# A decoder block on one core: the first loads of a product issued inside the unit before it, and its left factors written in portions between the weight splits

## The chip, the cores and the metric

The program runs on one core of a Trainium2 chip. TensorE (PE in the profile) multiplies matrices, VectorE (DVE), ScalarE (ACT) and GpSimd (POOL) work elementwise, and SyncE (SP) issues nearly all DMA transfers. Each of these works through its own list of instructions in order, and waits on semaphores for the others. The metric is the device time of one execution, in microseconds (us).

## The reference

One hybrid decoder block over 512 positions with 2048 features, in float32. Cut to what is computed:

```
h = rmsnorm(x, norm_mix_g);  z = h @ w_in                    # q, k, v, forget gates, zu, zv
attn = forgetting_attention(q, k, v, log_sigmoid(f + b_f))   # 8 heads, causal softmax
gm   = gelu(zu) * (tril(w_s) @ layernorm(gelu(zv)) + b_s)    # chunks of 128 positions
merged = concat(rmsnorm(attn, attn_out_g), rmsnorm(gm, gmlp_out_g))
x = x + merged @ w_out
h2 = rmsnorm(x, norm_ffn_g)
x = x + square(relu(h2 @ w_ff1)) @ w_ff2                     # 2048 -> 8192 -> 2048
return rmsnorm(x, norm_final_g)
```

The change is at the seam between `merged @ w_out` and `h2 @ w_ff1`, the first product of the channel MLP.

## The kernel before

Every float32 operand is written as a high part that TensorE takes exactly and a low part, the rest: ScalarE casts the high part, VectorE subtracts it from the source. A product is then three matmuls, high by high, high by low, low by high.

**Projection units.** The projections are cut into units of 128x512 weight tiles; `run_units` walks through their steps. A step prepares the weights of three steps ahead (load, `wh` on ScalarE, `wl` on VectorE), issues 12 matmuls of 128x512 into four PSUM tiles, calls the unit's `done` after its last step, and then `tick()`, which gives background tasks their turn: a task is a generator, and the number that it yields is how many ticks it sleeps. The last eight units multiply by `w_out`: `oa0` to `oa3` for the attention half, then `og0` to `og3`, whose `g_done(c)` adds both halves to x and so makes the features 512c to 512c+511 of the block's middle x, called `oa[c]`.

**The first channel product** (`first_product`, 448 groups) is a Strassen-Winograd product with seven partial products P1 to P7. Its left factors are seven forms (A11, A12, A22, S1 to S4) of the middle x, made for every c by `scale_x2(c)` (4 scalings on ScalarE, 4 sums on VectorE) and `make_forms(c, which)` (for each form one cast `L699` on ScalarE and one subtraction `L700` on VectorE). Its right factors are blocks of `w_ff1`, loaded by `load(u, j)` in four DMAs: `b11`, `r`, and the sums `t1` and `t3`, which the background task `sums_task` has made earlier (lines `L668` to `L674`) and put in DRAM. `prepare(i)` splits one weight block for one group: cast `fh` (`L723`) and subtraction `fl` (`L724`). A group is 12 matmuls of 128x256 on `L791`. The order of the groups in one j is P5, P1, P6, P2, P7, P4, P3. The groups of j = 0 and 1 read the forms of c = 0 and 1, those of j = 2 the forms of c = 2, those of j = 3 the forms of c = 3. In this text P7' is group P7 of j = 1.

**The seam.** `g_done(3)` first starts `first_product`, whose first part loads the blocks of j = 0 and 1 and prepares three groups; then it reads the four PSUM tiles of `og3` (`L614`, `L615`), scales, and makes the five remaining forms of c = 2 and all seven of c = 3. `turn_x2(c)` is a task that transposes `oa[c]` on TensorE (`px`, `L636`), copies it out on ScalarE and stores it; for c = 2 its first two pieces fall into `og3`, the rest between groups of the first product.

**What sets the order.** TensorE's order is that of the program. On the other engines a scheduler arranges the instructions when the kernel is built, by its own estimate of when operands come. SP's queue is in order too: a DMA that waits for its buffer holds all later ones. The buffers that matter: `t2_pool` (7 tiles; `b11`, `t1`, `t3`, the products of `L614`, the transposed copies), `raw_pool` (4; weights of the units and `r`), `w_pool` (4 `wh` and 4 `wl`, shared by units and groups, so that the split of a group waits for the matmuls of the step or group four before), and the six PSUM tiles of `ps_mm`. By their order of allocation the tile of P5 is the one that `px` 0 of c = 2 used, that of P1 the one of `px` 1; `px` 2 takes the tile `ps_og3_0` and must wait until VectorE has read it in the first `L614`; P6, P2 and P7 take `ps_og3_1`, `_2` and `_3` likewise.

Of the kernel before, what the change touches and what calls it, by code (L numbers as in the profile page):

```python
# [34 lines left out]
def hybrid_block(ctx, tc, xT, win, wf_in, wout, w1, w2, cols_in, ln_in, ws_in, out):  # L35
# [22 lines left out]
    def s8(name, dtype=F32, where=None):  # L58
        return (where or sr_pool).tile([P, 4, 512], dtype, tag="s8", name=name)

    def t2(name, dtype=F32):
        return t2_pool.tile([P, 512], dtype, tag="t2", name=name)
# [7 lines left out]
    def f(ap):  # L70
        return ap.bitcast(F32)
# [110 lines left out]
    tasks = []  # L182

    def start_task(gen, wait=1):
        tasks.append([wait, gen])
# [418 lines left out]
    def g_done(c):  # L604
        def done(ps):
            if c == 3:
                stage["first"] = first_product()
                next(stage["first"])
            if c == 2:
                oa[c] = s8(f"oa{c}")  # L610
            for m in range(4):
                k = 4 * c + m
                o, t = oa[c][:, m, :], t2(f"x2_{k}")
                nc.vector.tensor_tensor(t, ps[m], rG, ALU.mult)  # L614
                nc.vector.tensor_tensor(o, part[k], t, ALU.add)  # L615
            start_task(turn_x2(c), 6)
            scale_x2(c)
            if c < 2:
                make_forms(c, range(NF))
            elif c == 2:  # L620
                make_forms(c, (S1, A11))
            else:
                make_forms(2, (S2, A12, S3, A22, S4))
                make_forms(3, (S1, A11, S2, A12, S3, A22, S4))
        return done

    r2 = const.tile([P, NT], F32, name="r2")
    x2d = [dram.tile([P, NT, 512], F32, name=f"x2d{c}") for c in range(4)]

    def turn_x2(c):  # L630

        for m in range(4):
            xt = t2(f"x2t{c}_{m}")
            pt = mm(f"px{c}_{m}") if c > 1 else ax(f"px{c}_{m}", m % 2)
            for tb in range(NT):
                nc.tensor.transpose(pt[:, tb * P:(tb + 1) * P], oa[c][:, m, tb * P:(tb + 1) * P], ident)  # L636
            nc.scalar.copy(xt, pt)
            nc.sync.dma_start(out=x2d[c][:, :, m * P:(m + 1) * P], in_=xt.rearrange("p (t c) -> p t c", c=P))
            yield 2


    NF = 7
    A11, A12, A22, S1, S2, S3, S4 = range(NF)
# [3 lines left out]
    first = (P5, P1, P6, P2, P7, P4, P3)  # L647
    fac = [dram.tile([NF, P, 1024], F32, name=f"fac{u}") for u in range(NU)]
    stage = {}
    here = tc.keep_in_program_order  # L650

    def pairs(t):
        return t.rearrange("p (q c) -> p q c", q=2)
# [5 lines left out]
    def w1_block(u, j, c, n):  # L659

        return w1[8 * u + 2 * j:8 * u + 2 * j + 2][:, :, c:c + n].rearrange("q p c -> p q c")
# [18 lines left out]
    def scale_x2(c):  # L680
        xg, sx = (s8(f"{n}{c}", F32, sx_pool if c > 1 else None) for n in ("xg", "sx"))
        for m in range(4):
            k = 4 * c + m
            nc.scalar.activation(xg[:, m, :], oa[c][:, m, :], AF.Copy, scale=cols[:, G_FFN + k:G_FFN + k + 1])
        xv = xg.rearrange("p (i r) c -> p r i c", r=2)
        a11, a12, a21, a22 = (xv[:, r, :, t:t + 256] for t in (0, 256) for r in range(2))
        s1, s2, s3, s4 = (pairs(sx[:, i, :]) for i in range(4))
        nc.vector.tensor_tensor(s1, a21, a22, ALU.subtract)
        nc.vector.tensor_tensor(s2, s1, a11, ALU.subtract)
        nc.vector.tensor_tensor(s3, a11, a21, ALU.subtract)  # L690
        nc.vector.tensor_tensor(s4, a12, s2, ALU.add)
        x2g[c] = [a11, a12, a22, s1, s2, s3, s4]

    def make_forms(c, which):
        for i in which:
            if c % 2 == 0:
                forms[i, c // 2] = (sr_pool if c // 2 else sl_pool).tile([P, 4, 2, 256], F32R, tag="s8", name=f"form{i}_{c}")
            t = forms[i, c // 2][:, 2 * (c % 2):2 * (c % 2) + 2]
            nc.scalar.copy(t[:, :, 0, :], x2g[c][i])  # L699
            nc.vector.tensor_tensor(t[:, :, 1, :], x2g[c][i], f(t[:, :, 0, :]), ALU.subtract)  # L700


    def first_product():
# [3 lines left out]
        def load(u, j):  # L707
            if u >= NU:
                return
            b11, t1, t3 = (pairs(t2(f"{n}_{u}{j}")) for n in ("b11", "t1", "t3"))  # L710
            r = raw_pool.tile([P, 2, 512], F32, tag="raw", name=f"r{u}{j}")
            nc.sync.dma_start(out=b11, in_=w1_block(u, j, 0, 256))
            nc.sync.dma_start(out=r, in_=w1_block(u, j, 512, 512))
            nc.sync.dma_start(out=t1, in_=pairs(t1d[u][j]))
            nc.sync.dma_start(out=t3, in_=pairs(t3d[u][j]))
            blocks[u, j] = {P1: b11, P2: r[:, :, 0:256], P3: r[:, :, 256:512], P4: t1, P5: t1, P6: t1, P7: t3}
# [50 lines left out]
                square(b0)  # L767

        load(0, 0)
        load(0, 1)  # L770
        for i in range(3):
            prepare(i)
# [2 lines left out]
        for i, (u, j, p) in enumerate(groups):  # L775
# [9 lines left out]
            for q in range(2):  # L785
                ah, al = a[:, 2 * (j % 2) + q, 0, :], a[:, 2 * (j % 2) + q, 1, :]
                for m in range(2):
                    c = slice(q * 256 + m * P, q * 256 + (m + 1) * P)
# [323 lines left out]
    def g_unit(c):  # L1112
        unit(f"og{c}", wout, 8 * c + 4, 8, G_OUT + 8,
             lambda k: (gm_h[k // 4][:, k % 4, :], gm_l[k // 4][:, k % 4, :]), True, g_done(c))
# [62 lines left out]
```

## Time and profile before

| | |
|---|---|
| three runs | 2018.1 us median (2017.93 to 2018.88) |
| profiled execution | 2020.05 us, of which its trace spans 2018.2 us |
| TensorE busy | 1974.2 us, 98% |
| VectorE busy | 1598.8 us, 79% |
| ScalarE busy | 1052.4 us, 52% |
| GpSimd busy | 84.4 us, 4% |
| granted TensorE clock, mean | 0.991 |

A busy time is the sum of an engine's instructions; matmuls overlap, so TensorE at 98% still tells little about one place. The page's row of 40 slices has TensorE below nine tenths in two neighbouring slices only, the 14th and 15th, and its granted clock below nine tenths in the 15th; a slice is 50.5 us. The views of that stretch, in order of time, say which wait ended last.

### The profile page before, as it was taken

Reading aid. Unit: us, or ns where it says so; the run is one execution under the profiler, and the core shown is the slowest. Engines: PE = TensorE matmul, PEld = TensorE weight load, DVE = VectorE, ACT = ScalarE, POOL = GpSimd, SP = SyncE. Lnnn points to the kernel's source line nnn. Section 1 sums busy time; section 2 is a strip of 40 time slices with the busy share of each in tenths; the row PEclk is TensorE's granted clock in tenths of the full one; section 3 lists DMA queues with packets and bytes.
Section 4 is the critical chain, followed back from the end, with each engine's and each line's share of the span. In section 5 each row is a group of like instructions: output and inputs, shape, how many; then the busy total and the mean of one; then the engine's idle time right before and its main releaser. Section 6 shows DMA issues by size and latency. Waiting matters only on the chain.

```text
span 2018.2 us, 30643 instructions
## 1 busy us (share of the span) xinstructions
PE 1974.2 (98%) x11288; PEld 1729.7 (86%) x11288; DVE 1598.8 (79%) x2400; ACT 1052.4 (52%) x1692; POOL 84.4 (4%) x84
## 2 busy tenths in 40 slices
PE   9999999999999889999999999999999999999997
PEld 6888887888787689999999999997888888888876
DVE  7467566686667579988888888888888998998897
ACT  6344334445424456666666666666644444444455
POOL 5000001100120000000000000000000000000000
PEclk9999999999999989999999999999999999999998
DMA  6465565667766768987667756778956646646632
GB/s 220 150 200 160 192 196 171 206 208 256 235 198 204 241 196 291 323 288 234 196 218 244 234 194 219 242 260 313 354 179 218 229 154 230 242 136 237 246 122 84
DMA packets 226406, 439.91 MB, mean 218 GB/s; under 512 B 18896, under 2 KB 96848, under 8 KB 226128
## 3 DMA queue, kind: packets, MB, share of 16 engines
q1 hardware_dynamic: 225568, 436.09, 64.2%
q8 instruction: 88, 1.44, 0.3%
q10 hardware_dynamic: 432, 1.35, 0.2%
q0 software_dynamic: 256, 0.52, 0.1%
q14 instruction: 62, 0.51, 0.1%
HBM read 337.22 MB, written 100.66 MB: 217 GB/s over the span
## 4 chain that ended last, share of the span: by engine, by line
PE 62%; DVE 3%; issue 1%; DMA 1%; ACT 1%; SPq 0%; POOLq 0%; POOL 0%; DVEq 0%; ACTq 0%
PE q L791 32%; PE bX L1067 16%; PE bZ L1067 8%; PE bY L1067 4%; DVE wl L885 1%; PE ps_og L152 1%; PE ps_og L150 1%; PE ps_og L151 1%; DVE acc L946 0%; DVE acc L913 0%; PE px L636 0%; PE pt L970 0%; DVE acc L914 0%; DMA t<-t1d 0%; DVE raw L878 0%
## 5 line engine op out<-in xcount | busy, mean ns | idle before, releaser
L791 PE MATMUL q<-form,fh 128*128 128x256 f32 x3584 | 650.9, 284 | 8.4 <-ACT fh L723 8.4
L791 PEld LDWEIGHTS q<-form,fh 128*128 128x128 f32 x3584 | 562.7, 193 | 8.8 <-ACT fh L723 8.8
L791 PE MATMUL q<-form,fl 128*128 128x256 f32 x1792 | 510.3, 285 | 8.9 <-DVE fl L724 8.7
L791 PEld LDWEIGHTS q<-form,fl 128*128 128x128 f32 x1792 | 345.9, 193 | 10.6 <-DVE fl L724 10.0
L884 ACT CAST wh<-raw 128x1024 fp32r<-128x1024 f32 x224 | 234.4, 1054 | 222.7 <-PE bX L1067 122.4
L885 DVE TENSOR_TENSOR wl<-raw,wh 128x1024 fp32r<-128x1024 f32 x224 | 271.1, 1223 | 74.1 <-ACT wh L884 73.2
L1067 PE MATMUL bX<-wh,fac 128*128 128x512 f32 x1008 | 323.5, 394 | 3.7 <-ACT k_wl L905 2.1
L724 DVE TENSOR_TENSOR fl<-t,fh 128x512 fp32r<-128x512 f32 x256 | 176.4, 690 | 79.0 <-ACT fh L723 77.8
L1067 PEld LDWEIGHTS bX<-wh,fac 128*128 128x128 f32 x1008 | 190.6, 189 | 52.1 <-ACT k_wh L905 6.3
L723 ACT CAST fh<-t 128x512 fp32r<-128x512 f32 x256 | 158.2, 618 | 122.1 <-PE q L791 87.5
L1067 PE MATMUL bX<-wl,fac 128*128 128x512 f32 x504 | 199.3, 395 | 1.9 <-DVE wl L885 1.9
L1067 PE MATMUL bZ<-wh,fac 128*128 128x512 f32 x512 | 162.8, 389 | 0.0
L1067 PEld LDWEIGHTS bX<-wl,fac 128*128 128x128 f32 x504 | 95.4, 189 | 25.6 <-DVE wl L885 7.1
L1067 PEld LDWEIGHTS bZ<-wh,fac 128*128 128x128 f32 x512 | 96.1, 188 | 19.9
L723 ACT CAST fh<-r 128x512 fp32r<-128x512 f32 x128 | 79.1, 618 | 48.1 <-PE q L791 46.5
L150 PE MATMUL ps_qk<-xh,wh_qk 128*128 128x512 f32 x256 | 101.6, 397 | 0.0
L152 PE MATMUL ps_qk<-xh,wl_qk 128*128 128x512 f32 x256 | 100.0, 391 | 0.0
L151 PE MATMUL ps_qk<-xl,wh_qk 128*128 128x512 f32 x256 | 99.8, 390 | 0.0
L1067 PE MATMUL bZ<-wl,fac 128*128 128x512 f32 x256 | 99.6, 389 | 0.0
L724 DVE TENSOR_TENSOR fl<-r,fh 128x512 fp32r<-128x512 f32 x128 | 88.3, 690 | 11.6 <-ACT fh L723 11.0
L162 ACT ACTIVATE wh_qk<-raw_qk,cols 128x512 fp32r<-128x512 f32 x64 | 46.3, 724 | 94.6 <-PE ps_qk L151 62.9
L163 DVE SCALAR_TENSOR_TENSOR wl_qk<-raw_qk,cols,wh_qk 128x512 fp32r<-128x512 f32 x64 | 47.7, 750 | 59.0 <-ACT wh_qk L162 58.9
(618 smaller groups left out, 3567.3 us busy)
## 6 DMA issues: line engine op xcount, KB each, us to landing
b<-in_w_dram SPq DMA_DIRECT2D x256, 256.0 KB, 4.3
raw<-in_w_dram SPq DMA_DIRECT2D x128, 512.0 KB, 4.9
fac<-fac SPq DMA_DIRECT2D x112, 512.0 KB, 6.2
r<-in_w_dram SPq DMA_DIRECT2D x64, 512.0 KB, 5.5
fac<-fc SPq DMA_DIRECT2D x48, 512.0 KB, 4.2
raw_qk<-in_win_dram SPq DMA_DIRECT2D x32, 512.0 KB, 3.8
t1d<-b SPq DMA_DIRECT2D x64, 256.0 KB, 2.1
t3d<-b SPq DMA_DIRECT2D x64, 256.0 KB, 2.3
```

Of the source, the lines that this page charges most:

```text
L150: nc.tensor.matmul(ps, lhsT=ah, rhs=bh, start=start, stop=False)
L151: nc.tensor.matmul(ps, lhsT=ah, rhs=bl, start=False, stop=False)
L152: nc.tensor.matmul(ps, lhsT=al, rhs=bh, start=False, stop=stop)
L162: nc.scalar.activation(wh, raw, AF.Copy, scale=g)
L163: nc.vector.scalar_tensor_tensor(wl, raw, g, f(wh), ALU.mult, ALU.subtract)
L723: nc.scalar.copy(pairs(wh), b[p])
L724: nc.vector.tensor_tensor(pairs(wl), b[p], pairs(f(wh)), ALU.subtract)
L791: nc.tensor.matmul(d, lhsT=l[:, c], rhs=r, start=j == 0 and q == 0 and m == 0 and w == 0, stop=j == 3 and q == 1 and w == 2, skip_group_ch ...
L884: nc.scalar.copy(wh, s)
L885: nc.vector.tensor_tensor(wl, s, f(wh), ALU.subtract)
L1067: nc.tensor.matmul(banks[chain][t], lhsT=l, rhs=r, start=start and w == 0, stop=stop and w == 2, skip_group_check=True)
```

## The change

`g_done(2)` now makes the generator of `first_product` and hands it to the ticks with a sleep of 3, so that its first `load` is issued in the second step of `og3`. The generator then yields 1000, and `g_done(3)` takes it out of the list of tasks and resumes it: it loads j = 1, and prepares three groups as before. The forms that `g_done(3)` made at once are made by a new task, `last_forms`, in six portions, one at each tick: first the forms of c = 2 in two, then those of c = 3 in four, with `scale_x2(3)` ahead of these.

```diff
             if c == 3:
-                stage["first"] = first_product()
+                tasks[:] = [t for t in tasks if t[1] is not stage["first"]]
                 next(stage["first"])
             if c == 2:
                 oa[c] = s8(f"oa{c}")
+                stage["first"] = first_product()
+                start_task(stage["first"], 3)
...
             start_task(turn_x2(c), 6)
-            scale_x2(c)
-            if c < 2:
-                make_forms(c, range(NF))
-            elif c == 2:
-                make_forms(c, (S1, A11))
+            if c < 3:
+                scale_x2(c)
+                make_forms(c, range(NF) if c < 2 else (S1, A11))
             else:
-                make_forms(2, (S2, A12, S3, A22, S4))
-                make_forms(3, (S1, A11, S2, A12, S3, A22, S4))
+                start_task(last_forms())
         return done
+
+    def last_forms():
+
+        make_forms(2, (S2, A12))
+        yield 1
+        make_forms(2, (S3, A22, S4))
+        yield 1
+        scale_x2(3)
+        for which in ((S1, A11), (S2, A12), (S3, A22), (S4,)):
+            yield 1
+            make_forms(3, which)
...
         load(0, 0)
+        yield 1000
         load(0, 1)
```

Line numbers after the change are higher by 2 for the reads of PSUM (`L614` becomes `L616`), by 10 from `turn_x2` to the splits (`L700` becomes `L710`, `L724` becomes `L734`) and by 11 for the groups. TensorE's instructions stand in the same order in both kernels.

SP's queue at the seam, before (`b1230` to `b1232` and `b1210`, `b1212` belong to the sums, `x2d` is a store of a transposed piece, `b11_00`, `t1_00`, `t3_00` are the first loads of j = 0, `..._01` those of j = 1):

```order
L668 DMA b1231_6277<-in_w1_dram 128x2x256
L638 DMA x2d2_154<-x2t2_1_6294 512x1x128
L668 DMA b1230_6276<-in_w1_dram 128x2x256
L668 DMA b1232_6278<-in_w1_dram 128x2x256
L712 DMA b11_00_6314<-in_w1_dram 128x2x256
L714 DMA t1_00_6315<-t1d0_172 128x512
L715 DMA t3_00_6316<-t3d0_188 128x512
L712 DMA b11_01_6322<-in_w1_dram 128x2x256
L714 DMA t1_01_6323<-t1d0_172 128x512
L715 DMA t3_01_6324<-t3d0_188 128x512
```

The same queue now, where the loads of j = 0 stand:

```order
L171 DMA raw_og3_6_6226<-in_wout_dram 128x1024
L723 DMA r01_6325<-in_w1_dram 128x2x512
L648 DMA x2d1_153<-x2t1_2_6162 512x1x128
L722 DMA b11_00_6194<-in_w1_dram 128x2x256
L724 DMA t1_00_6195<-t1d0_172 128x512
L725 DMA t3_00_6196<-t3d0_188 128x512
L723 DMA r02_6441<-in_w1_dram 128x2x512
L648 DMA x2d1_153<-x2t1_3_6218 512x1x128
L683 DMA t1d12_184<-b1210_6061 128x512
L684 DMA t3d12_200<-b1212_6063 128x512
```

The three loads of j = 0 moved up from behind the store of piece 1 of c = 2 to behind the store of piece 2 of c = 1. The load `raw_og3_6`, weights of `og3` itself, changed places with `r00`, the fourth load of j = 0: it stands seven rows later than before.

VectorE ahead of the split of P7 of j = 0, before (`form3_2` is form 3 in the tile that begins at c = 2, here its half of c = 3; forms 0 to 6 are A11, A12, A22, S1, S2, S3, S4):

```order
L700 TENSOR_TENSOR form3_2_6132<-sx3_6357,form3_2_6132 128x2x256
L691 TENSOR_TENSOR sx3_6357<-xg3_6356,sx3_6357 128x512
L700 TENSOR_TENSOR form4_2_6366<-sx3_6357,form4_2_6366 128x2x256
L700 TENSOR_TENSOR form1_2_6369<-xg3_6356,form1_2_6369 128x2x256
L700 TENSOR_TENSOR form5_2_6372<-sx3_6357,form5_2_6372 128x2x256
L700 TENSOR_TENSOR form2_2_6375<-xg3_6356,form2_2_6375 128x2x256
L700 TENSOR_TENSOR form6_2_6378<-sx3_6357,form6_2_6378 128x2x256
L670 TENSOR_TENSOR b1230_6276<-b1230_6276,b1231_6277 128x512
L671 TENSOR_TENSOR b1232_6278<-b1232_6278,b1231_6277 128x512
L724 TENSOR_TENSOR fl00_7_6415<-t3_00_6316,fh00_7_6414 128x512
L724 TENSOR_TENSOR fl00_4_6442<-t1_00_6315,fh00_4_6441 128x512
L724 TENSOR_TENSOR fl00_3_6459<-r00_6317,fh00_3_6458 128x512
```

VectorE around the same split now:

```order
L740 TENSOR_TENSOR t1_00_6195<-t1_00_6195,r00_6197 128x512
L734 TENSOR_TENSOR fl00_2_6365<-r00_6197,fh00_2_6364 128x512
L710 TENSOR_TENSOR form2_2_6411<-xg2_6122,form2_2_6411 128x2x256
L710 TENSOR_TENSOR form6_2_6414<-sx2_6123,form6_2_6414 128x2x256
L734 TENSOR_TENSOR fl00_7_6382<-t3_00_6196,fh00_7_6381 128x512
L616 TENSOR_TENSOR x2_12_6344<-ps_og3_0_6144,rG_150 128x512
L616 TENSOR_TENSOR x2_13_6347<-ps_og3_1_6145,rG_150 128x512
L617 TENSOR_TENSOR oa3_5493<-oa3_5493,x2_12_6344 128x512
L617 TENSOR_TENSOR oa3_5493<-oa3_5493,x2_13_6347 128x512
L616 TENSOR_TENSOR x2_14_6350<-ps_og3_2_6146,rG_150 128x512
L616 TENSOR_TENSOR x2_15_6353<-ps_og3_3_6147,rG_150 128x512
L617 TENSOR_TENSOR oa3_5493<-oa3_5493,x2_14_6350 128x512
```

The split of P7 moved ahead of the reads of `og3`'s PSUM tiles; the forms of c = 3 that stood before it are gone from here, and the splits of P5, P1, P6 and P2 stand ahead of all these rows.

VectorE in j = 1, before:

```order
L724 TENSOR_TENSOR fl01_6_6533<-t1_01_6323,fh01_6_6532 128x512
L730 TENSOR_TENSOR t1_01_6323<-t1_01_6323,r01_6325 128x512
L724 TENSOR_TENSOR fl01_2_6551<-r01_6325,fh01_2_6550 128x512
L670 TENSOR_TENSOR b1300_6483<-b1300_6483,b1301_6484 128x512
L671 TENSOR_TENSOR b1302_6485<-b1302_6485,b1301_6484 128x512
L724 TENSOR_TENSOR fl01_7_6569<-t3_01_6324,fh01_7_6568 128x512
L724 TENSOR_TENSOR fl01_4_6585<-t1_01_6323,fh01_4_6584 128x512
L724 TENSOR_TENSOR fl01_3_6611<-r01_6325,fh01_3_6610 128x512
```

VectorE in j = 1 now, from the same split:

```order
L734 TENSOR_TENSOR fl01_6_6523<-t1_01_6323,fh01_6_6522 128x512
L734 TENSOR_TENSOR fl01_2_6541<-r01_6325,fh01_2_6540 128x512
L740 TENSOR_TENSOR t1_01_6323<-t1_01_6323,r01_6325 128x512
L680 TENSOR_TENSOR b1300_6459<-b1300_6459,b1301_6460 128x512
L681 TENSOR_TENSOR b1302_6461<-b1302_6461,b1301_6460 128x512
L710 TENSOR_TENSOR form4_2_6358<-sx3_6466,form4_2_6358 128x2x256
L710 TENSOR_TENSOR form1_2_6361<-xg3_6465,form1_2_6361 128x2x256
L734 TENSOR_TENSOR fl01_7_6563<-t3_01_6324,fh01_7_6562 128x512
L734 TENSOR_TENSOR fl01_4_6579<-t1_01_6323,fh01_4_6578 128x512
L710 TENSOR_TENSOR form5_2_6408<-sx3_6466,form5_2_6408 128x2x256
L710 TENSOR_TENSOR form2_2_6411<-xg3_6465,form2_2_6411 128x2x256
L734 TENSOR_TENSOR fl01_3_6609<-r01_6325,fh01_3_6608 128x512
```

Here the forms of c = 3 came in: S2 and A12 ahead of the split of P7', S3 and A22 ahead of that of P3'.

## Rows read from the trace of the kernel before

**Rows 1.** The page: span, busy times, TensorE's clock in slices, the groups' matmuls.

```profile
span 2018.2 us, 30643 instructions
...
PE 1974.2 (98%) x11288; PEld 1729.7 (86%) x11288; DVE 1598.8 (79%) x2400; ACT 1052.4 (52%) x1692; POOL 84.4 (4%) x84
...
PEclk9999999999999989999999999999999999999998
...
L791 PE MATMUL q<-form,fh 128*128 128x256 f32 x3584 | 650.9, 284 | 8.4 <-ACT fh L723 8.4
```

**Rows 2.** Busy time by stretch: length, then PE, PEld, DVE, ACT, POOL; PEclk, DMA.

```profile
620.00:640.00 20.00, 18.72 (x83) 15.15 (x83) 17.02 (x28) 10.97 (x18) 0.00 (x0) 1.00 0.41 137
...
700.00:710.00 10.00, 3.83 (x16) 3.53 (x17) 3.99 (x7) 2.72 (x5) 0.00 (x0) 0.56 0.62 209
710.00:720.00 10.00, 5.48 (x39) 5.07 (x38) 9.30 (x16) 8.37 (x16) 0.00 (x0) 0.84 0.08 26
720.00:730.00 10.00, 6.11 (x34) 6.11 (x35) 7.43 (x13) 1.92 (x4) 0.00 (x0) 0.58 0.77 238
```

**Rows 3.** TensorE in order of time: start, length, instruction, [idle before <- releaser].

```profile
696.99 0.39 PE L151 MATMUL ps_og<-gl,wh_og 128*128 128x512 f32 x1
697.22 0.39 PE L152 MATMUL ps_og<-gh,wl_og 128*128 128x512 f32 x1
706.03 0.58 PE L791 MATMUL q<-form,fh 128*128 128x256 f32 x1 [8.43 <-ACT fh L723]
...
714.57 0.39 PE L791 MATMUL q<-form,fl 128*128 128x256 f32 x1 [0.78 <-DVE fl L724]
...
723.89 0.58 PE L791 MATMUL q<-form,fl 128*128 128x256 f32 x1 [7.63 <-DVE fl L724]
```

**Rows 4.** The chain that ended last: start, length, what.

```profile
706.76 5.05 PE q L791 x23
...
729.35 5.76 PE q L791 x48
...
741.29 0.44 PE px L636 x4
```

**Rows 5.** SP's queue in order of time.

```profile
666.47 0.58 SPq L171 DMA_DIRECT2D raw_og<-in_wout_dram  x1
...
673.89 0.47 SPq L713 DMA_DIRECT2D r<-in_w_dram  x1
...
678.92 0.53 SPq L638 DMA_DIRECT2D x2d<-x2t  x1
...
698.88 0.49 SPq L712 DMA_DIRECT2D b<-in_w_dram  x1
699.47 0.41 SPq L714 DMA_DIRECT2D t<-t1d  x1
```

**Rows 6.** ScalarE in order of time.

```profile
682.40 0.72 ACT L162 ACTIVATE wh_og<-raw_og,cols 128x512 fp32r<-128x512 f32 x1 [1.99 <-PE ps_og L151]
...
705.36 0.62 ACT L723 CAST fh<-t 128x512 fp32r<-128x512 f32 x1 [6.81 <-DMA t<-t1d]
```

**Rows 7.** VectorE in order of time.

```profile
693.51 0.69 DVE L670 TENSOR_TENSOR b<-b,b 128x512 f32<-128x512 f32 x1 [2.45 <-DMA b<-in_w_dram]
695.20 0.69 DVE L671 TENSOR_TENSOR b<-b,b 128x512 f32<-128x512 f32 x1 [1.00 <-DMA b<-in_w_dram]
...
720.74 0.69 DVE L700 TENSOR_TENSOR form<-xg,form 128x512 fp32r<-128x512 f32 x1
721.34 0.69 DVE L700 TENSOR_TENSOR form<-sx,form 128x512 fp32r<-128x512 f32 x1
```

**Rows 8.** DMA issues from 640 to 760 us: KB each, median us to landing.

```profile
b<-in_w_dram SPq DMA_DIRECT2D x33, 256.0 KB, 4.2
...
raw_og<-in_wout_dram SPq DMA_DIRECT2D x5, 512.0 KB, 4.7
```

**Rows 9.** The line that loads the sums' blocks, whole trace.

```profile
DMA to landing us min/median/max: 2.8/4.3/6.8
```

## Prediction, written before the changed kernel ran

> **What bounds the kernel now.** I read the page first: TensorE is busy for 1974.2 of 2018.2 us, so at most some 44 us are to be had from it, and its granted clock falls at one place in the middle and at the very end [rows 1]. The busy times by stretch then show that the place is the seam: between 700 and 730 us TensorE is busy for 3.83, 5.48 and 6.11 us of 10 each, at a mean clock of 0.56, 0.84 and 0.58 [rows 2]. TensorE in order of time shows three waits there: 8.43 us for the first group P5, until a cast of ScalarE; 0.78 us for a subtraction of VectorE; and 7.63 us for another, in P7 [rows 3]. The chain of waits shows the groups themselves: 23 matmuls take 5.05 us right behind the first long wait, and as many take as long behind the second, while 48 take 5.76 us later [rows 4]; so a matmul costs 0.120 us at 2.4 GHz and 0.22 us in those stretches, which is the 1.2 GHz level.
>
> The first wait ends last on a load: the cast of P5 waited 6.81 us for `t1` [rows 6], issued at 699.47, after TensorE was through with `og3` [rows 5]. The second ends on VectorE: the split of P7 comes behind a row of forms and sums that run without a pause, one every 0.60 us (720.74, 721.34) [rows 7]. The forms there belong to c = 3, which is not read before j = 3.
>
> **The mark.** TensorE's order is unchanged, so I compare when it reaches the transpose behind the 14 groups of j = 0 and 1: 741.29 us before [rows 4]. The last matmul of `og3` began at 697.22, 0.23 us after the one before it [rows 3], so TensorE could begin something else at 697.45; from there it is 43.84 us. The work in it is 14 x 12 matmuls at 0.120 = 20.16 us and three transposes at 0.44 = 1.32 us [rows 4], in all 21.48. So 22.4 us are lost: 8.43 + 0.78 + 7.63 = 16.8 in waits and about 5.5 in clock. That is the most that the change can return.
>
> **The loads.** In SP's new order the loads of `b11_00`, `t1_00`, `t3_00` stand behind the store that went out at 678.92, and the one before it, `r01`, has its time already. I put them at 679.5 to 681; even if they took the 6.81 us for which the cast of P5 waited before [rows 6], they would be there by 688, 9 us ahead of P5. The price of the exchange: `raw_og3_6` moves from 666.47 to 673.89 [rows 5], lands 4.7 us later [rows 8] at 678.6, and its cast at 682.40 waited for TensorE, not for the load [rows 6]: cost 0, with 3.8 us of cover. The queue behind is held up by three issues of about 0.5 us each [rows 5]: the stores and sums there serve the first product, and I put that at 0; without that cover it is 1.5 us.
>
> The splits of P5, P1 and P6 then wait only for `w_pool`, that is for the fifth, sixth and seventh step of `og3`. ScalarE does them beside `og3`; P5 and P1 are ready, and the 8.43 us go to 0, with the slow 23 matmuls behind it: 5.05 - 23 x 0.120 = 2.3 us. VectorE has the sums `b` between the splits of P1 and P6, which now hold it until 695.89 (695.20 + 0.69) [rows 7]; P6 is not wanted before 700.
>
> **VectorE from P7 on.** This is what comes late next. The `fh` of P7 takes the buffer of P5, so its cast starts when P5 ends: 697.45 + 11 x 0.120 + 0.28 (length of one matmul [rows 1]) = 699.05. The cast takes 0.62 [rows 6], and `fl` of P7 starts at 699.75. From here VectorE's new order is a row without a gap until `fl` of P3', 33 places later; at 0.60 us a place (the step of [rows 7]) I walk it against TensorE:
>
> - The read of `ps_og3_0` stands one place behind `fl` of P7: 700.35 to 701.04. The transpose needs its PSUM tile; TensorE ends P1 at 697.45 + 24 x 0.120 = 700.33, and waits 0.77.
> - P6 and P2 need the next two tiles (reads at 2 and 5 places: done at 701.64 and 703.44): waits 0.16 and 0.36. P7 needs none.
> - `fl` of P4 stands 11 places behind, after two sums: done at 707.04, while P4 would go on with its second matmul at 706.5: wait 0.60. P3 ends at 710.30 with the transpose between.
> - In j = 1 three of the four sums of `scale_x2(3)` stand ahead of `fl` of P5' (16 places); P5' does not wait, P1' 0.04, P6' 0.38 (22 places, 713.64 against 713.3). P7' (29 places, behind two sums and two forms) is ready at 717.84 against 716.96: 0.90. P4' and P3' do not wait (30 and 33 places).
>
> The new waits sum to 0.77 + 0.16 + 0.36 + 0.60 + 0.04 + 0.38 + 0.90 = 3.2 us, and TensorE is at the mark at 697.45 + 21.48 + 3.2 = 722.1. From j = 2 on VectorE has 7 splits, 2 sums, 2 sums of the background task and one form per 10.1 us, that is 12 x 0.60 = 7.2, and falls behind no more. Gain: 741.29 - 722.1 = 19.2 us. Later stages keep their order, and nothing in them waits for the seam.
>
> No row of before shows the sums `b` waiting in this place with the new queue, so I bound that wait: below, 0, since TensorE cannot run faster than without waits; above, by the waits of 2.45 and 1.00 us that they had at 693.51 and 695.20 [rows 7]. Of three such pairs the first has 5 us of cover. The second (ahead of `fl` of P4) I put as issued at 697 to 699 and landed 4.2 us later [rows 8] at 703, wanted at 705.15; the third (ahead of P7') landed at 714.0, wanted at 715.35. With the longest landing of that line, 6.8 us [rows 9], the second is 0.2 us late and the third 0.8. I take 0, the nearest to the median landing, and keep 0 to 3.5 us.
>
> The sum, made against the profiled execution: 2020.05 (span 2018.2 and 1.85 around it) - 19.2 = 2000.9. The median of the three runs, 2018.1, is 1.95 below the profiled one; 2018.1 - 19.2 = 1998.9. I predict 1999.0.
>
> **Rivals.** *The clock falls again.* TensorE no longer stands still for 8 us, but it stops seven times in 21 us. For: each of the two long waits was followed by the 1.2 GHz level. Against: the wait of 0.78 us at 714.57 was not (the next matmuls start 0.12 us apart), and between 620 and 640 us TensorE was idle for 20 - 18.72 = 1.28 us while the clock stayed at 1.00 [rows 2, 3]. But no row shows seven in a row. One or two falls cost 2.3 us each, as before [rows 4]: 2001.2 to 2003.5. The Trainium skill (TensorE: Matmul & The Clock Gate, section A second HAM failure mode: psum-queue depth-cycling) describes just this: frequent small pauses between groups, as TensorE goes from one PSUM bank to the next, let the clock go back and forth and lower the throughput. No run here shows it so far: by that rule the time is this rival's, by the rows on single short waits the forecast's.
>
> *The loads stay late, or the sums hold VectorE.* If SP's first load waits for a buffer of `t2_pool` that comes free only when `og3` ends, `t1` is issued near 698.0 instead of 699.47 [rows 5]: the first wait shrinks by 1.5 us only and keeps its slow matmuls, the second (7.63 and 2.3 of clock) and the 0.78 still go, less the 3.2 of new waits: 1.5 + 10.7 - 3.2 = 9.0 us of gain, 2009. Sums that hold VectorE as long as in [rows 7] give 1998.9 + 3.5 = 2002.4. For: the order lists a wait of this load for GpSimd and TensorE, without saying for which instruction. Against: the ring's tiles that come free for it were last used in `og2` or earlier, whose reads are over when the store at 678.92 goes out [rows 5].
>
> *Slower: the low clock stays.* If TensorE, always a little behind VectorE, is held at 1.2 GHz while the backlog lasts and beyond, a group costs 12 x (0.22 - 0.12) = 1.2 us more, and 19.2 us are used up after 16 groups; with all 28 groups of the first u it is 14 us slower, 2032. No row speaks for it; against it stands that each fall before ended after some 5 us of matmuls [rows 4], though VectorE was busy for 9.30 and 7.43 us of 10 around them [rows 2].
>
> **How the numbers follow.** Forecast (gain of 17 to 22 us) 0.77; the clock falls once or twice 0.11; loads or sums late 0.07; low clock that stays 0.03; the rest, a gain lost for a cause that I don't see, 0.02. A change of less than 0.2%, 4 us, is about what measurement cannot tell from none. Faster: 0.77 + 0.11 + 0.07 = 0.95, from which I take 0.01 for late loads that cost more; same 0.03; slower 0.03. The range begins at no new waits, 2018.1 - 22.4 = 1995.7, and reaches over the falling clock to 2004.
>
> **What would show it.** Right: the first load of `t1` before 682 us; the first group within 0.5 us of the last matmul of `og3`; no wait of TensorE over 1.2 us until the mark, most of them for VectorE; the clock at 1.00 throughout; the mark at 722 us. Wrong: a cast of P5 that waits for a DMA; a clock below 0.9 between 695 and 725; `fl` of P4 or P7' behind a sum that waits for its block; a wait of `og3` for `raw_og3_6`.

## The result and the profile after

Five runs of the changed kernel had a median of 2000.99 us (1999.39 to 2002.97), five of the kernel before beside them 2018.1 us (2015.93 to 2022.7). The ratio is 0.9912, with a 95% interval of 0.9899 to 0.9924: faster by 17.1 us, where 19.1 were forecast. Run beside the kernel before twice more (table below), the changed kernel was 19.5 and 20.4 us faster by the medians (2019.96 to 2000.51, 2019.76 to 1999.34). The profiled execution took 2002.97 us, the longest of the five, of which its trace spans 2001.3.

The page after (its parts as in [rows 1]):

```profile
span 2001.3 us, 30641 instructions
...
PE 1966.3 (98%) x11288; PEld 1721.9 (86%) x11288; DVE 1597.4 (80%) x2400; ACT 1051.7 (53%) x1692; POOL 84.1 (4%) x84
...
PEclk9999999999999999999999999999999999999999
...
L802 PE MATMUL q<-form,fh 128*128 128x256 f32 x3584 | 647.4, 283 | 1.0 <-DVE x L616 1.0
```

The dip of the clock in the middle is gone, and so is the wait of 8.4 us for `fh` at the groups' line. Busy time by stretch, the columns as in [rows 2]:

```profile
690.00:700.00 10.00, 10.00 (x53) 8.46 (x53) 7.44 (x13) 3.89 (x7) 0.00 (x0) 1.00 0.86 267
700.00:710.00 10.00, 7.95 (x61) 7.14 (x61) 9.27 (x16) 6.75 (x13) 0.00 (x0) 1.00 0.74 219
710.00:720.00 10.00, 9.23 (x76) 8.81 (x74) 10.00 (x18) 7.40 (x14) 0.00 (x0) 1.00 0.90 302
720.00:730.00 10.00, 10.00 (x83) 10.00 (x84) 9.19 (x16) 4.11 (x7) 0.00 (x0) 1.00 0.95 309
```

From 700 to 730 us TensorE is busy for 27.18 us where it was for 15.42, at a clock of 1.00 throughout. In order of time (columns as in [rows 3]), with every wait that the view lists between `og3` and the mark:

```profile
698.28 0.39 PE L152 MATMUL ps_og<-gh,wl_og 128*128 128x512 f32 x1
698.50 0.28 PE L802 MATMUL q<-form,fh 128*128 128x256 f32 x1
...
702.33 0.66 PE L646 MATMUL px<-ident,oa 128*128 128x128 f32 x4 [0.79 <-DVE x L616]
...
703.75 0.39 PE L802 MATMUL q<-form,fh 128*128 128x256 f32 x1 [0.77 <-DVE x L616]
...
705.65 0.36 PE L802 MATMUL q<-form,fh 128*128 128x256 f32 x1 [0.20 <-DVE x L616]
...
709.16 0.38 PE L802 MATMUL q<-form,fl 128*128 128x256 f32 x1 [0.29 <-DVE fl L734]
...
720.00 0.39 PE L802 MATMUL q<-form,fl 128*128 128x256 f32 x1 [0.65 <-DVE fl L734]
```

The first group starts where `og3` ends, at 698.50, without a wait. `og3` itself ends 1.06 us later than before; the units ahead of it are unchanged, and in ten other executions with these units as they were it ended between 696.57 and 699.00, so this belongs to the run. SP's queue shows why P5 no longer waits, ScalarE that the casts wait for TensorE and not for a load (columns as in [rows 5, 6]):

```profile
675.49 0.47 SPq L171 DMA_DIRECT2D raw_og<-in_wout_dram  x1
...
679.99 0.53 SPq L648 DMA_DIRECT2D x2d<-x2t  x1
680.61 0.57 SPq L722 DMA_DIRECT2D b<-in_w_dram  x1
681.28 0.41 SPq L724 DMA_DIRECT2D t<-t1d  x1
```

```profile
683.47 0.72 ACT L162 ACTIVATE wh_og<-raw_og,cols 128x512 fp32r<-128x512 f32 x1 [1.99 <-PE ps_og L151]
...
689.34 0.62 ACT L733 CAST fh<-t 128x512 fp32r<-128x512 f32 x1 [0.96 <-PE ps_og L151]
```

`t1` is issued at 681.28 instead of 699.47, and `raw_og`, which now goes out later, is still not what the cast at 683.47 waits for. The wait that the prediction's sum lacks is in VectorE's order of time and in the chain (columns as in [rows 7, 4]):

```profile
700.99 0.68 DVE L734 TENSOR_TENSOR fl<-t,fh 128x512 fp32r<-128x512 f32 x1
701.59 0.68 DVE L616 TENSOR_TENSOR x<-ps_og,rG 128x512 f32<-128x512 f32 x1
703.01 0.69 DVE L616 TENSOR_TENSOR x<-ps_og,rG 128x512 f32<-128x512 f32 x1 [0.73 <-DMA x2d<-x2t]
```

```profile
698.05 4.94 DMA x2d<-x2t
...
703.01 0.69 DVE x L616
...
724.47 0.44 PE px L646 x4
```

The second read of `og3`'s PSUM waits 0.73 us, not for TensorE, but for a store: its product goes to a tile of `t2_pool` that still holds a transposed piece, and the store of that piece, issued at 698.05, lands 4.94 us later. Behind it VectorE works without a gap to 724.

The mark: 724.47 - 698.51 = 25.96 us after TensorE was through with `og3`, against 43.84 before [rows 3, 4]. The seam gives 17.88 us. The rest of the way of the span, 2018.2 - 2001.3 = 16.9, is the run's 1.06 us ahead of the seam, 1.1 given back between the mark and the second product, and 1.2 gained behind that (before, the clock fell once more near 1974 us; after, not at that place).

### The profile page after: what moved, and what is told of

Its sections match the earlier page's. It is cut to its first block, busy times and chain, and to the rows that moved or that the text cites. A ratio compares the mean times of both kernels' runs of the same rounds, so it can differ in the third digit from the quotient of the medians.

```text
span 2001.3 us, 30641 instructions
## 1 busy us (share of the span) xinstructions
PE 1966.3 (98%) x11288; PEld 1721.9 (86%) x11288; DVE 1597.4 (80%) x2400; ACT 1051.7 (53%) x1692; POOL 84.1 (4%) x84
## 3 DMA queue, kind: packets, MB, share of 16 engines
q8 instruction: 88, 1.44, 0.3%
## 4 chain that ended last, share of the span: by engine, by line
PE 58%; DVE 5%; DMA 3%; issue 1%; ACT 1%; SPq 0%; POOLq 0%; POOL 0%; DVEq 0%; ACTq 0%
PE q L802 28%; PE bX L1078 16%; PE bZ L1078 7%; PE bY L1078 4%; DMA b<-in_w_dram 1%; DVE wl L896 1%; PE ps_og L152 1%; PE ps_og L150 1%; PE ps_og L151 1%; DVE fl L734 1%; DMA x2d<-x2t 1%; DMA x2l<-x2d 0%; DVE acc L957 0%; DVE acc L924 0%; DMA t1d<-b 0%
## 5 line engine op out<-in xcount | busy, mean ns | idle before, releaser
L734 DVE TENSOR_TENSOR fl<-t,fh 128x512 fp32r<-128x512 f32 x256 | 176.2, 690 | 68.0 <-ACT fh L733 66.8
L734 DVE TENSOR_TENSOR fl<-r,fh 128x512 fp32r<-128x512 f32 x128 | 88.2, 689 | 10.1 <-ACT fh L733 9.4
```

Of the source, the lines that this page charges most:

```text
L734: nc.vector.tensor_tensor(pairs(wl), b[p], pairs(f(wh)), ALU.subtract)
```

## The experiments

All are made from the changed kernel. The table has the device time, the interval of the ratio to the kernel before, which ran anew beside each group of versions, and two stretches from the profiled execution, both beginning where TensorE is through with `og3`: to the mark, by its start in order of time (the chain puts it 0.16 us later), and to the first matmul of the second product.

| kernel | median us (runs, range) | ratio | mark | 2nd product |
|---|---|---|---|---|
| before | 2018.1 (5, 2015.93 to 2022.7) | | 43.68 | 671.76 |
| changed | 2000.99 (5, 1999.39 to 2002.97) | 0.9899 to 0.9924 | 25.81 | 655.00 |
| changed, again | 2000.51 (4, 1999.57 to 2000.78) | 0.9883 to 0.992 | 25.40 | 653.22 |
| changed, third | 1999.34 (4, 1998.3 to 2002.7) | 0.9882 to 0.9912 | 27.24 | 655.79 |
| early loads only | 2010.26 (5, 2007.84 to 2011.17) | 0.9934 to 0.9969 | 30.64 | 659.67 |
| portions only | 2011.81 (7, 2007.7 to 2014.26) | 0.9943 to 0.9977 | 36.81 | 665.45 |
| sums paused | 2001.98 (6, 1999.25 to 2005.05) | 0.99 to 0.993 | 22.98 | 655.20 |
| tiles of their own | 2004.29 (1) | | 26.38 | 654.26 |
| held once | 2003.69 (1) | | 28.19 | 656.68 |
| all sums early | 2012.44 (12, 2007.86 to 2017.08) | 0.9949 to 0.9973 | 22.45 | 648.71 |
| the same, own tiles, reads first | 2010.54 (6, 2006.51 to 2014.65) | 0.9937 to 0.9972 | 21.44 | 648.66 |
| paused, own tiles, reads first | 1998.81 (4, 1996.71 to 2000.04) | 0.9879 to 0.9911 | 21.45 | 650.39 |
| the same, again | 1997.13 (5, 1996.47 to 2005.55) | 0.988 to 0.9915 | 21.45 | 653.04 |
| the same, half of the sums early | 1997.82 (5, 1995.41 to 2000.8) | 0.9875 to 0.9909 | 21.44 | 648.98 |

**Each half alone.** Early loads, with the forms made at once as before:

```diff
-            if c < 3:
-                scale_x2(c)
-                make_forms(c, range(NF) if c < 2 else (S1, A11))
+            scale_x2(c)
+            if c < 2:
+                make_forms(c, range(NF))
+            elif c == 2:
+                make_forms(c, (S1, A11))
             else:
-                start_task(last_forms())
+                make_forms(2, (S2, A12, S3, A22, S4))
+                make_forms(3, (S1, A11, S2, A12, S3, A22, S4))
```

> Only the first half of the change: the loads of j = 0 are issued in the second step of og3, but all forms are made at once as before. My theory (two waits with two causes, each with its own fall of the clock): the first wait (8.43 us) and the slow matmuls behind it are gone, a long wait for VectorE remains, now at P3 instead of P7, since the split of P3 stands 14 places behind that of P4, or 8.4 us: a wait of 6 to 7 us and 2.3 us of slow clock. The mark behind 14 groups comes 31 to 33 us after og3's last matmul, against 43.8 before and 26.0 with the whole change; time 2005 to 2007 us. Rival theory (the early loads are the whole gain, the portions only move work about): the time of the whole change, 2001 us, and no wait over 1 us.

And the portions, with the loads at the end of `og3` as before:

```diff
-                tasks[:] = [t for t in tasks if t[1] is not stage["first"]]
+                stage["first"] = first_product()
...
-                stage["first"] = first_product()
-                start_task(stage["first"], 3)
...
-        yield 1000
```

> Only the second half: the forms in six portions, the loads of j = 0 issued at the end of og3 as before. My theory: the first wait stays at 8 to 9 us, ends on the load of t1, and is followed by some 5 us at 1.2 GHz; the wait of 7.63 us is gone, in its place a wait of about 2 us at P2, whose split stands 15 places behind that of P5. The mark comes 34 to 36 us after og3's last matmul; time 2008 to 2010 us. Both halves alone would then return more together than the whole change, because VectorE works off part of its backlog during the first wait. Rival theory (the portions alone take all waits away, since the scheduler finds a better order): 2001 us.

The one long wait of TensorE that the first has left:

```profile
714.58 0.58 PE L805 MATMUL q<-form,fl 128*128 128x256 f32 x1 [5.63 <-DVE fl L737]
```

and the two of the second:

```profile
705.49 0.58 PE L799 MATMUL q<-form,fh 128*128 128x256 f32 x1 [8.77 <-ACT fh L731]
...
715.23 0.39 PE L799 MATMUL q<-form,fl 128*128 128x256 f32 x1 [2.60 <-DVE fl L732]
```

Without the portions the wait for VectorE's forms comes later, at P3, and is 5.63 us instead of 7.63; without the early loads the wait for the load stays whole and that for VectorE shrinks to 2.60. To the mark, the loads alone give 13.0 us and the portions alone 6.9; both together give 17.9, so the two halves go against two different waits and nearly add. Their sum, 19.9, is 2 us more than the whole, as the second expectation had it. The marks came out at the edge of what was expected (30.6 for 31 to 33, 36.8 for 34 to 36); the medians are higher than expected in both, by 2 to 5 us; the kernel before had a median of 2019.78 beside them, 1.7 more than the 2018.1 of the first comparison.

**The bounded sums out of the seam.**

```diff
             if c == 2:
+                next(t for t in tasks if t[1] is stage["sums"])[0] += 16
...
-    start_task(sums_task(), 18)
+    stage["sums"] = sums_task()
+    start_task(stage["sums"], 18)
```

> The whole change, and the background task that makes the sums sleeps 16 ticks longer from the end of og2, so that none of its loads, stores and sums falls into the seam (they are done later, and all are done). My theory (VectorE's row of splits, forms and sums is what TensorE waits for, so each place taken out of it ahead of a split comes back): four sums fewer between the split of P7 and that of P3', and the reads of og3's PSUM tiles come first; waits of TensorE in the seam sum to 0.8 to 1.5 us instead of 4.5, the mark comes 22.3 to 23 us after og3's last matmul instead of 26.0; time 1997 to 1999 us. Rival theory (the waits come from the buffers, of the splits in w_pool and the stores of transposed pieces, not from VectorE's number of places): no more than 1 us less than with the whole change, mark at 25 us or later.

The mark came as expected, 22.98, 2.8 us ahead of the changed kernel's. Without the sums' loads in SP's queue the store of the transposed piece goes out at 696.43 instead of 698.05. VectorE still waits 0.65 us for it, but is done with that read at 701.69, and P6 starts at 701.75, at most 0.13 us late. TensorE's only listed waits to the mark are 0.71 us at 707.15 and 0.18 at 713.77. But the second product starts no earlier, and the time, 2001.98, missed the 1997 to 1999 of the expectation. Where the 3 us went is in TensorE's order of time after the seam, three rows of it:

```profile
826.67 0.38 PE L803 MATMUL q<-form,fl 128*128 128x256 f32 x1 [0.40 <-DVE fl L735]
...
830.27 0.39 PE L803 MATMUL q<-form,fl 128*128 128x256 f32 x1 [0.47 <-DVE fl L735]
...
833.88 0.39 PE L803 MATMUL q<-form,fl 128*128 128x256 f32 x1 [0.47 <-DVE fl L735]
```

Two more stand at 860.52 and 872.77 and one of 0.65 at 1347.86. What VectorE waited for between 735 and 900 us (line, releaser: us in total, times, longest), paused and then not paused:

```profile
DVE b L681 <- DMA b<-in_w_dram: 10.3, 6, 2.3
```

```profile
DVE b L680 <- DMA r<-in_w_dram: 2.3, 1, 2.3
DVE b L680 <- DMA b<-in_w_dram: 1.8, 2, 1.2
```

The postponed sums run on to 896 us instead of 849, and the DMA engines are busy for 0.96 of 780 to 900 us (0.90 in the changed kernel), and VectorE waits 10.3 us for their loads, where it was 4.4 in this execution of the changed kernel and 2.6 and 2.9 in the two others. The seam's gain turned into waits 100 us later.

**Own tiles for the four products.** This takes the store out of the way by giving the products another buffer.

```diff
-                o, t = oa[c][:, m, :], t2(f"x2_{k}")
+                o = oa[c][:, m, :]
+                t = t2(f"x2_{k}") if c < 3 else const.tile([P, 512], F32, tag=("ssum", "nF")[m % 2], name=f"x2_{k}")
```

> The whole change, but the four products that read og3's PSUM tiles are put into two tiles of their own instead of the ring in which one of them waits for a store. My theory: the read of the second tile no longer waits 0.7 us for a store, and the scheduler puts all four reads ahead of the splits of P2 and P7, but with two sums of the background task between, whose last block lands near 706 us: so the first two waits of TensorE (0.79 and 0.77 us) vanish and a wait of 3 to 4 us at P2 comes, and the mark is 26 to 28 us after og3's last matmul. Rival theory (the store's wait is what costs): the mark at 25 us.

```profile
706.00 0.50 PE L803 MATMUL q<-form,fl 128*128 128x256 f32 x1 [3.17 <-DVE fl L735]
```

As my theory had it: `px` and P6 wait no more, but the scheduler now sets all reads and two sums ahead of the split of P2, and the wait is there, longer, with matmuls at 1.2 GHz behind it. Of the 3.17 us, 1.36 are the two sums' own waits for their loads (0.71 and 0.65). The mark, 26.38, is no earlier. Since the order moved with the buffer, this run alone does not price the store.

**One single wait, made by hand.** VectorE goes six times over the first PSUM tile of `og3` before it reads it.

```diff
+            for _ in range(6 if c == 3 else 0):
+                nc.vector.tensor_scalar(ps[0], ps[0], 1.0, None, ALU.mult)
```

> The whole change, and VectorE goes six times over the first PSUM tile of og3 (times 1.0, in place) before it reads it, so that TensorE waits there once for about 4.3 us, with matmuls at the full clock before and after. Theory: the clock of before fell because of single waits of 7.6 us and more; after a wait of 4 us the granted clock either falls for about 5 us of matmuls (mark some 4.3 + 2.3 us later: 32 to 33.5 us after og3's last matmul) or stays at 1.00 (mark 29.5 to 31). Rival (the clock fell for another reason than the waits, such as VectorE's or the DMAs' standstill): no matmul of 0.5 us after this wait.

```profile
705.00 1.12 PE L648 MATMUL px<-ident,oa 128*128 128x128 f32 x4 [4.03 <-DVE x L618]
705.77 0.56 PE L804 MATMUL q<-form,fh 128*128 128x256 f32 x1
```

The matmul behind it has 0.56 us, and the ten from 705.77 to 707.99 take 2.22 us instead of 1.20: the lower level, for a shorter stretch than in [rows 4]. So one wait of 4 us is enough, while VectorE works on (7.84 of the 8 us from 696 to 704) and the DMA engines too (a share of 0.75); the rival, by which no slow matmul would follow, is refuted. The mark came out earlier than either case expected, since the long wait takes the place of four short ones: 4.2 for it, 1.0 for the clock in the groups and 0.4 in the transposes, less 3.1 (0.95, 1.18, 0.43, 0.54 in the table of waits below), and the mark is 2.4 later.

**All sums behind the kernel before the seam.** Each sum takes three ticks, not four.

```diff
                 here(nc.sync.dma_start(out=t3d[u][j], in_=b22))
-                yield 1
```

> The whole change, and each bounded weight sum takes three ticks, not four, so that all 64 sums are behind the kernel before the last projection unit: none stands among VectorE's operations of the seam, and none loads between 700 and 850 us, where the DMA engines are busiest. Theory A (what the postponed sums gained at the seam was given back because their loads came into a stretch with full DMA engines): here the seam's gain stays; the mark 24 to 25.3 us after og3's last matmul (the store's hold on ps_og3_1 stays), no wait for fl at 850 us, time 1997 to 2000 us. Theory B (VectorE's order after the seam, not the loads, took it back, or the end of the kernel does): the mark as early, but the time stays at 2000 to 2002.5. If the crowding before 700 us costs TensorE waits: 2002 to 2006.

The same, with own tiles, and the reads emitted ahead of the first splits of j = 1:

```diff
             if c == 3:
                 tasks[:] = [t for t in tasks if t[1] is not stage["first"]]
-                next(stage["first"])
...
                 nc.vector.tensor_tensor(o, part[k], t, ALU.add)
+            if c == 3:
+                next(stage["first"])
```

> As the one before, and the four products that read the PSUM tiles of og3 write to tiles of their own (no store of a transposed piece is in the way) and stand ahead of the first weight splits of the next portion. Theory A: no wait at the first px, one of 0 to 1.2 us at P2's low part (nine VectorE operations at 0.60 us behind fl of P6, beside 4 us of matmuls), the mark 22.3 to 23.5 us after og3's last matmul, time 1995 to 1998 us, which would be below both kernels. Theory B: mark as early, time 2000 to 2002.

Both times missed every case. Behind `og3` all went better than expected: no wait at all to the mark in the second (21.44 us, which is the work alone), and the second product after 648.7 us, 4.5 to 7.1 less than in the three executions of the changed kernel. But `og3` ended at 713.69 and 713.42 us, 15 to 16 late. Two waits of TensorE that are new there, of the first of the two (columns as above):

```profile
PE ps_og L150 <- DVE oa L600: 2.3, 1, 2.3
PE ps_oa L150 <- DVE oa L600: 2.0, 1, 2.0
```

Up to 680 us TensorE is idle for 7.4 us more in all than in the changed kernel, and its mean clock, 1.00 there, is 0.97 from 300 to 400 us, 0.99 from 500 to 620 and 0.98 from 620 to 680, which costs some 5 more; some 2 more are not accounted for. More sums per step came between the projection units' own work on VectorE; the price that I had named for it, 2002 to 2006 us, was too low.

**Pause, own tiles, reads first.** The edits are those above, together.

> The whole change; the bounded sums pause for 16 more ticks from the end of og2's products, so none stands in the seam; the four products on og3's PSUM tiles write to tiles of their own and stand ahead of the first weight splits of the next portion. Both theories: the mark 22.3 to 23.3 us after og3's last matmul, no wait at the first px, 0 to 1 us at P2's low part. Theory A (what is gained at the seam is given back where the postponed sums load, in a stretch with full DMA engines): TensorE waits 2 us or more in all for low parts between 780 and 900 us, time 2000 to 2002.5 us. Theory B (it was the order of the postponed sums alone in one run): those waits under 1 us, time 1996.5 to 1999.

```profile
700.00:710.00 10.00, 10.00 (x87) 10.00 (x86) 9.72 (x17) 8.41 (x16) 0.00 (x0) 1.00 0.53 163
710.00:720.00 10.00, 10.00 (x86) 10.00 (x86) 9.84 (x17) 6.66 (x13) 0.00 (x0) 1.00 0.54 154
```

TensorE has no gap left at the seam. The waits for low parts between 780 and 900 us were 0.47 us in all, as the theory without a price for the pause had it, and the time, 1998.81, lies in its range. Beside the changed kernel on one chip:

> The changed kernel beside the next one on one chip: 2000 to 2001.5 us. From og3's last matmul to the second product's first one 653 to 655 us.

> The version without bounded sums in the seam, with tiles of their own and the reads of og3's PSUM tiles first, again, beside the changed kernel on one chip. If what it gained at the seam (4 us) is kept: 1997 to 1998.5 us, 2 to 4 us below the changed kernel, and 650 to 651 us from og3's last matmul to the second product. If the waits of 2.8 us between 820 and 900 us that the pause alone showed come back: 653 us there, and 2000 to 2002 us.

The changed kernel came out just outside both of its ranges (1999.34, and 655.79 us). In the other version the medians came as in the first case, the profiled execution as in the second: the waits for low parts were 2.78 us (0.48, 1.31, 0.52, 0.47), VectorE waited 8.7 us for the sums' loads from 735 to 900 us, where it had been 5.2, and the second product came after 653.04 us. This execution was the longest of its five, 2005.55; 3.7 of the 7.3 us by which its span exceeds that of the first one lie behind the start of the second product, where its clock fell at four places. So the pause has its price in some executions and hardly in others. By medians of runs side by side this version is 2.2 us below the changed kernel, but the intervals of the two ratios overlap nearly whole; that it is faster is likely, not shown. The changed kernel had in its turn been measured again beside the versions with early sums:

> The changed kernel again, beside the next three on one chip, so that differences of 2 to 3 us can be told from runs of the same chip. Expected: 2001 us (1999 to 2003), the mark 26.0 us (25.5 to 26.5) after og3's last matmul, the read of ps_og3_1 held by the store by about 0.7 us again.

The mark came after 25.40 us, and the read was held for 0.34 us only.

**Half of the sums early.** As the version just named, and

```diff
-                yield 1
+                if u >= 8:
+                    yield 1
```

> As the one before, and each of the first 32 of the 64 bounded sums takes three ticks, not four, which moves them forward into the stretch of the first projection units, where the run with all sums early lost nothing in its first 300 us. The last sum then stands about 100 us earlier. Theory A: the mark as before (22.3 to 23.3 us after og3's last matmul), the waits for low parts between 780 and 900 us under 1 us in all, time 1996 to 1999 us, below both kernels, if the units before 500 us lose no more than 1 us. Theory B: no difference from the one before. If the earlier loads cost the projection units time, as the full version did between 300 and 680 us: 2001 to 2005.

The last sum is done earlier, the DMA share of 780 to 900 us falls to 0.79, VectorE's waits for the sums' loads from 735 to 900 us to 1.5 us, TensorE's for low parts to 0.25: this bears out that the loads were the price of the pause. From `og3` to the second product it takes 648.98 us, but some 4 us are lost ahead of `og3`'s end, at 701.49. Its median, 1997.82, is below both kernels, though the changed one did not run beside it, and it is not separated from the version before it.

## Why the prediction was right, and what was mis-sized

**The two long waits and the clock: right.** The first load of `t1` before 682 us (681.28), no wait at P5, none over 1.2 us to the mark, a clock of 1.00: each came as put in this execution and in the second. In the third the wait at P6 was 1.44 us and the clock fell (below, under the rivals). The price of the exchange with `raw_og3_6` was 0, as put.

The split of the 22.4 us is a little off: by the prediction's own 2.3 us a fall, the clock took 4.6 and not about 5.5. The rest are waits too, since a listed wait is short by 0.16 us (next paragraph) and P5's second matmul came 0.73 us behind its first (706.76 and 706.03 [rows 3, 4]).

**The new waits: 4.5 us, not 3.2.** A listed wait counts from the modelled end of the matmul before, 0.28 us after its start, while the next could have started after 0.12; so I take what the starts lose beside the steady 0.12 us:

| | `px` | P6 | P2 | P4 | P1' | P6' | P7' | sum |
|---|---|---|---|---|---|---|---|---|
| predicted | 0.77 | 0.16 | 0.36 | 0.60 | 0.04 | 0.38 | 0.90 | 3.2 |
| measured | 0.95 | 1.18 | 0.43 | 0.54 | 0.07 | 0.38 | 0.92 | 4.5 |

The walk along VectorE's order at 0.60 us a place held within 0.1 us at five of seven groups. The step that was mis-sized is "a row without a gap", and in it P6 (0.16): the order shows in which sequence VectorE works, and I checked for each place which splits and PSUM tiles were wanted, but not which buffer it writes. The product's tile had last been a transposed piece, whose store must land first. Of the 1.3 us, 1.0 is this place and 0.2 is `px`, where the row began 0.2 us later beside `og3`'s end than put (`fl` of P7 at 700.99 - 1.06 = 699.93 instead of 699.75).

The three profiled executions of the changed kernel have the same order, and the store's landing differs. The read was held for 0.34, 0.73 and 1.41 us, and TensorE waited 0.38, 0.77 and 1.44 us at P6 as listed: what holds the read is what P6 pays. The landing of 4.94 us is near the upper end (2.6 to 5.4 us for these stores, median 3.7). In the third execution SP was held for 1.88 us by a sum's load, and the store went out at 699.03:

```profile
702.64 0.69 DVE L616 TENSOR_TENSOR x<-ps_og,rG 128x512 f32<-128x512 f32 x1 [1.41 <-DMA x2d<-x2t]
```

**The bounded sums' wait: 0, as put.** P4 and P7', behind the second and third pair of sums, are within 0.06 us of a forecast that had nothing for them. The bound beside it was misreckoned: with a landing of 6.8 us the second pair is 0.45 us late (703 + 2.6 against 705.15) and the third 1.25 (714.0 + 2.6 against 715.35), not 0.2 and 0.8; neither is in the sum. That VectorE does not wait for the sums' loads in the seam is true only while they stay where they are: see the pause, and the version with own tiles. And through SP's queue a sum's load can delay the store, as in the third execution.

**"Later stages keep their order, and nothing in them waits for the seam": 1.1 us off.** From the mark to the second product the profiled execution took 1353.50 - 724.31 = 629.19 us, before 1369.21 - 741.13 = 628.08. A wait of 0.98 us at 850.83 was new, for a low part behind a sum that had waited 2.34 us for a load; the two other executions took 627.82 and 628.55.

**The rivals.** *The clock falls again* came true in one of the three profiled executions of the changed kernel. In the first two the clock stayed at 1.00 over the short waits, each 0.79 us or less as listed. In the third, TensorE waited 0.79 and 1.44 us within 3 us, and from 704 to 706 and 706 to 708 us the granted clock was 0.62 and 0.53, the lower level for some 3.6 us, then 1.00 again:

```profile
703.39 0.39 PE L802 MATMUL q<-form,fh 128*128 128x256 f32 x1 [1.44 <-DVE x L616]
...
705.84 0.63 PE L802 MATMUL q<-form,fh 128*128 128x256 f32 x2
...
708.18 0.40 PE L802 MATMUL q<-form,fh 128*128 128x256 f32 x2
```

It cost less than the 2.3 us of the rival: from the first matmul of P6 to the transpose behind P4 it took 7.43 us (703.39 to 710.82) instead of 6.83 in both others, since the waits at P2 and P4 fell into it. The Trainium skill's rule on frequent small pauses between groups (TensorE: Matmul & The Clock Gate, section A second HAM failure mode: psum-queue depth-cycling) would have had the clock go back and forth. It did so in one execution of three; what decides between them, no run here shows. Single waits of 2.60 us and more in the versions above (2.60, 3.17, 4.03, 5.63, 8.77) were each followed by the lower level at the seam. The late loads and the low clock that stays are refuted by the rows on SP and by the clock.

Of the difference of 2.0 us to the median, 1.3 is the new waits; the rest, 0.7, is no more than the medians of the changed kernel differ among themselves (1999.34 to 2000.99). Since two later comparisons gave 19.5 and 20.4 us for the forecast 19.1, the miss in the time is within what separates one comparison from the next; the one at P6 is shown by the traces.

## What to carry to other kernels

Where an engine's order is walked place by place, each place has three questions: are its inputs there, is its result wanted, and who still reads the buffer that it writes; a DMA store out of a ring of buffers is such a reader until it lands, here for 2.6 to 5.4 us. What is moved out of a crowded stretch must be priced where it arrives: postponed sums came back as late loads, sums made earlier as waits of the projection units. At the seam a long wait of TensorE cost itself and the slow matmuls behind it, so one of 8 us was worth turning into many short ones here; that short ones leave the clock alone held in two executions of three.

## What was not expected of the hardware

After waits of the same length the clock did not always do the same. Some 25 us after its first matmul the second product waits for 2.1 us in every kernel. Behind it, in the profiled execution of the changed kernel and in its second one, TensorE in order of time:

```profile
1378.60 0.50 PE L1078 MATMUL bX<-wh,fac 128*128 128x512 f32 x1 [2.11 <-ACT k_wl L916]
...
1380.00 1.05 PE L1078 MATMUL bX<-wh,fac 128*128 128x512 f32 x2
```

```profile
1376.27 0.50 PE L1078 MATMUL bX<-wh,fac 128*128 128x512 f32 x1 [2.11 <-ACT k_wl L916]
...
1377.53 0.62 PE L1078 MATMUL bX<-wh,fac 128*128 128x512 f32 x2
```

In the first, pairs of matmuls take 1.05 us from 1380.00 on, the lower level, until some 3 us later; in the second they take 0.62 throughout. Of the fourteen profiled executions of all versions, ten fell to the lower level behind this wait and four did not. In the version with all sums early, a wait of 1.99 us at 544 us was followed by it and one of 2.29 us at 617 us was not. A wait of 3.50 us near the end of the kernel left the clock at 1.00 in the profiled execution of the changed kernel (32 transposes in 4.05 us) and was followed by 0.50 in its second (the same 32 in 6.65). So for waits of 1.99 to 3.50 us the length alone does not tell. I estimate one such fall at 1.7 us (from 1378 to 1384 us the granted clock was 0.92, 0.50 and 0.73 in stretches of 2 us); that a part of the spread of one kernel's runs comes from it is likely, not shown.
